# RWKV state chain as batched affine maps, chunk matrices of two heads in one loop, full-height lora products

## The chip, the cores and the metric

The kernel runs on one core of a Trainium2 chip. The metric is the device time of one execution in microseconds, the median of three runs. The profile is one more execution on the same core; its engines are named PE (matrix multiply), PEld (PE's weight loads), DVE, ACT and POOL (element-wise work) and SP (which issues the DMAs).

## The reference

Two layers over x of shape (1, 512, 1024). In each layer one projection of the normalised input is split among three token mixers: latent attention (8 heads), forgetting attention (8 heads) and RWKV-7 time mixing (8 heads of 64). Their gated outputs are projected, merged and added to x. The change lies in the RWKV mixer, whose core is a recurrence over the 512 positions with a 64 by 64 state for each head:

```python
def step(state, inp):
    r_t, w_t, k_t, v_t, kk_t, a_t = inp
    sa = jnp.einsum('bhvk,bhk->bhv', state, -kk_t)
    state = (state * w_t[:, :, None, :] + sa[..., None] * (kk_t * a_t)[:, :, None, :]
             + v_t[..., None] * k_t[:, :, None, :])
    return state, jnp.einsum('bhvk,bhk->bhv', state, r_t)
```

The decay w and the rate a come from two small products ("lora") with 64 inner values each; in the second layer v is mixed with the first layer's v through a third one with 32 inner values.

## The kernel before

Everything is written with features on the 128 partitions and the 512 positions along the free axis. The large products are made of 128 by 128 weights against 128x512 moving tiles in three passes (`mm3`: high by high, high by low, low by high, all float32r), and weights are split into high and low parts on ACT, DVE and POOL as they arrive. Each layer is written as five generators that are woven together: `rwkv_preps`, `rwkv_chains`, `attention`, `merge_gates`, `merge`. The instructions that come out of them are then put in an order by the function `plan`, which lists, for each engine, the instructions in the order in which the engine will issue them; it weighs the path that is left behind an instruction and prices of its own for each kind of instruction, waits and changes of PE's tile shape. Some copies may go to one of two or three engines, and `plan` picks. On the chip each engine keeps that order, so PE issues work of all five generators in turn, and a matmul that waits holds all that is listed behind it.

The RWKV mixer treats the heads in four pairs per layer (the index p; head 0 of a pair lies on partitions 0 to 63, head 1 on 64 to 127, `HS` names both halves) and the positions in 8 chunks of 64. `rwkv_front` makes decay and rate: `lora` multiplies the weights `ws` by `WA` with one product over 128 rows and one over 64 rows. `rwkv_inv` makes the chunk matrices `At` for each head and chunk (L979, 16 products of `KB0` and `KR` per pair, for one head after the other, in the PSUM bank `xk`) and inverts their triangular part into `W` (a loop on POOL, and 32-row products at L1020 and L1026). `rwkv_chain` then walks the chunks. In the stretches that the prediction reads, one chunk is

- R: `Rs` = At part of head h times values (L1056), plus `KR` times the state `Sh` (L1065, not in chunk 0),
- A: `W` times `Rs` (L1069), copied into `VSA` as two 64x64 pieces,
- S: `KBn` times `VSA` (L1075, not in chunk 7), from which the next state is made on DVE (L1077) with the scaled old state `sl`.

Each of R, A and S is one 64 by 64 product for each of the two heads, side by side in different halves of the array, and each needs the result of the one before it, through DVE or ACT. The outputs follow at the end: for each chunk L1087 (128 rows, 64 columns) and, from chunk 1 on, L1093 (64 by 64). All these operands are plain float32, and the profile counts two PE instructions ("passes") for each such product. The PSUM bank `ch` has one buffer, so its users follow one another.

Of the kernel before, what the change touches and what calls it, by code (L numbers as in the profile page):

```python
# [9 lines left out]
F32 = mybir.dt.float32  # L10
# [203 lines left out]
def plan(insts, tags, manual, flex, margin, replay=None):  # L214
# [79 lines left out]
    short = [op.kind == "InstMatmult" and op.cost < 107 for op in ops]  # L294
# [4 lines left out]
    def forward(follow=None):  # L299
# [11 lines left out]
        table, columns, last_pass, last_short = "exp", [(0, 128)], 0.0, False  # L311
        held = [(0.0, 0)] * 5
        mode, pe_end = (128, 128), 0.0
# [94 lines left out]
        for _ in ops:  # L408
# [14 lines left out]
            if op.kind == "InstMatmult":  # L423
                last_short = short[k]
                c0, c1 = op.outs[0][1:3]
                load = op.array[1] / 1.2
                ld = max(due(k, e), last_pass)
                if op.array != mode:
                    ld = max(ld, pe_end + DRAIN)
                    mode = op.array  # L430
                s = max(s, ld + load)
                if c1 - c0 <= 64 and all(c1 <= a or b <= c0 for a, b in columns):
                    cost = 20
                    columns.append((c0, c1))
                    last_pass = s
                else:
                    columns = [(c0, c1)]
                    last_pass = s + (0 if "float32r" in op.ins[0][7] or op.inst.is_transpose else cost / 2)
            start[k], free[e] = s, s + cost
            if e == PE:  # L440
                pe_end = max(pe_end, s + dict(op.costs)[e])
# [90 lines left out]
def build(tc, x_t, wpk, wsm, wv, vec, cst, out, order_of=None, pick={}, queues=None, margin=2.0):  # L532
# [184 lines left out]
    for l in range(L):  # L717
# [160 lines left out]
        def load_v(p):  # L878
            v = T(tag="vp", bufs=2)
            nc.sync.dma_start(v, vs[p])  # L880
            if l:
                vu, u = TX(), T(dt=F32R)[:, 0:256].rearrange("p (a c) -> p a c", a=2)
                nc.sync.dma_start(vu[64:128, 0:128], wv[l - 1, 64:128, 128 + 128 * p:256 + 128 * p])
                copy(u[64:128, 0, :], vu[64:128, 0:128])
                combine(u[64:96, 1, :], vu[64:96, 0:128], u[64:96, 0, :].bitcast(F32), ALU.subtract)
# [17 lines left out]
        def lora(ps, ws, i):  # L903

            pe.matmul(ps, ws[:, i, :], WA[:, i, :], start=True, stop=False)
            pe.matmul(ps, ws[HS[i], 2, :], WA[HS[i], i, :], start=False, stop=True)

        def rwkv_front(p):
# [4 lines left out]
            ws = T(dt=F32R)[:, 0:384].rearrange("p (i c) -> p i c", i=3)  # L913
            copy(ws[:, 0:2, :], raw[:, 0:256].rearrange("p (i c) -> p i c", i=2))
            for i, hs in enumerate(HS):
                combine(ws[hs, 2, :], raw[hs, 128 * i:128 * i + 128], ws[hs, i, :].bitcast(F32), ALU.subtract)
# [37 lines left out]
        def rwkv_inv(p, front, v):  # L954
# [19 lines left out]
            for h, hs in enumerate(HS):  # L974
                for g in range(2):
                    ps = PS("xk").rearrange("p (c t) -> p c t", t=128)
                    for c in range(4):
                        cc = 4 * g + c
                        pe.matmul(ps[:, c, :], KB0[hs, cc].rearrange("p a t -> p (a t)"),  # L979
                                  KR[hs, cc].rearrange("p a t -> p (a t)"), start=True, stop=True)  # L980
                    dve.tensor_tensor(At[:, h, 4 * g:4 * g + 4, :], ps,
                                      amask.unsqueeze(1).broadcast_to([128, 4, 128]), op=ALU.mult)
                    yield
# [47 lines left out]
        def rwkv_chain(p, ops):  # L1031
# [17 lines left out]
            built[0] += 1  # L1049
            Sh = rpool.tile([128, 8, 64], F32, name="Sh", tag="Sh", bufs=1)  # L1050
            for c in range(8):
                ps = PS("ch")
                pR, pA, pS = (ps[:, 64 * i:64 * i + 64] for i in range(3))
                Rs = T((128, 64), "Rs", 1)
                for h, hs in enumerate(HS):
                    pe.matmul(pR[hs], At[hs, h, c, 0:64], VSA[hs, c, hs], start=True, stop=c == 0)  # L1056
                if c:
                    if c < 7:
                        sl = T((128, 64), "sl", 1)
                        lc = lam[:, c:c + 1]  # L1060
                        any_of([(DVE, 162), (ACT, 240), (POOL, 472)], lambda q: act.activation(
                            sl, Sh[:, c, :], AF.Copy, scale=lc) if q == ACT else
                            (dve if q == DVE else gp).tensor_scalar(sl, Sh[:, c, :], lc, None, op0=ALU.mult))
                    for h, hs in enumerate(HS):
                        pe.matmul(pR[hs], KR[hs, c, 0, :], Sh[hs, c, :], start=False, stop=True)  # L1065
                copy(Rs, pR, DVE)
                yield
                for h, hs in enumerate(HS):
                    pe.matmul(pA[HS[1 - h]], W[hs, c, :], Rs[hs], start=True, stop=True)  # L1069
                for h, hs in enumerate(HS):  # L1070
                    copy(VSA[HS[1 - h], c, hs], pA[HS[1 - h]], DVE)
                yield
                if c < 7:
                    for h, hs in enumerate(HS):
                        pe.matmul(pS[hs], KBn[:, c, hs], VSA[:, c, hs], start=True, stop=True)  # L1075
                    if c:
                        dve.scalar_tensor_tensor(Sh[:, c + 1, :], pS, lam[:, c:c + 1], sl, op0=ALU.mult, op1=ALU.add)  # L1077
                    else:
                        dve.tensor_scalar(Sh[:, c + 1, :], pS, lam[:, c:c + 1], None, op0=ALU.mult)
                    yield  # L1080

            ps = PS("ch")
            last = [None, None]
            for c in range(8):
                cc = slice(64 * c, 64 * c + 64)
                for h, hs in enumerate(HS):
                    i1 = pe.matmul(ps[hs, cc], VSA[:, c, hs], At[:, h, c, 64:128], start=True, stop=c == 0)  # L1087
                    if c:
                        order(i1, last[h])
                    last[h] = i1  # L1090
                for h, hs in enumerate(HS):
                    if c:
                        last[h] = pe.matmul(ps[hs, cc], Sh[hs, c, :], KR[hs, c, 1, :], start=False, stop=True)  # L1093
# [640 lines left out]
```

## Time and profile before

| what | value |
|---|---|
| time, median of 3 runs | 1460.1 us (1458.55 to 1460.61) |
| time of the profiled execution | 1460.2 us |
| its span, first to last instruction | 1458.4 us |
| PE busy | 1409.8 us (97%), 7828 instructions |
| DVE busy | 1178.6 us (81%) |
| ACT busy | 787.9 us (54%) |
| POOL busy | 390.1 us (27%) |
| weight loads (PEld) busy | 1079.9 us (74%) |
| mean granted TensorE clock | 0.987 |
| DMA | 158.59 MB, mean 109 GB/s |

Busy time of PE counts a matmul from its start to its modelled end, and neighbours overlap: two 128x512 matmuls start 0.23 us apart and each lasts 0.39 us. What a piece of work costs PE is therefore read from starts: from the start of the matmul ahead of it to the start of the second matmul behind it, less what those two neighbours take when nothing lies between them.

### The profile page before, as it was taken

The numbers are of one execution on the slowest core, as the hardware profiler recorded it, in microseconds if no ns is written. First come the engines' busy times: TensorE is split into PE (matmuls) and PEld (weight loads), VectorE is DVE, ScalarE is ACT, GpSimd is POOL, SyncE is SP. The second block draws the span as 40 slices with busy tenths as digits, with TensorE's granted clock in tenths as the row PEclk, the third lists the DMA queues.
The fourth block names the chain that finished last, engine by engine and source line by source line (L and its number), as shares of the span: only waits on it lengthen the run. The fifth ranks groups of instructions, "written<-read, shape, count | busy, mean of one in ns | idle before, by whom it ended". The sixth has DMA issues, their size and how long they took to land. (4 is left out here: it accounts for less than half of the span.)

```text
span 1458.4 us, 23568 instructions
## 1 busy us (share of the span) xinstructions
PE 1409.8 (97%) x7828; PEld 1079.9 (74%) x7828; DVE 1178.6 (81%) x2787; ACT 787.9 (54%) x1653; POOL 390.1 (27%) x793
## 2 busy tenths in 40 slices
PE   7999999999999999999999999999989999999998
PEld 5677677676677777887877776777777676778887
DVE  8868878879887869878788778778688988688784
ACT  7546666546555546442254756457458567464330
POOL 1225260352440102112021251161252271012020
PEclk9999999999999999999999999999999999999999
DMA  5343123222333224555534332123232333254563
GB/s 172 109 120 105 44 59 88 80 62 84 94 80 116 88 79 139 166 184 166 184 116 130 93 97 65 55 64 103 84 95 58 122 85 95 66 174 152 164 211 102
DMA packets 114619, 158.59 MB, mean 109 GB/s; under 512 B 36544, under 2 KB 44608, under 8 KB 114496
## 3 DMA queue, kind: packets, MB, share of 16 engines
q1 hardware_dynamic: 114496, 157.08, 35.9%
q8 instruction: 62, 1.02, 0.3%
q14 instruction: 61, 0.50, 0.1%
HBM read 128.72 MB, written 28.31 MB: 108 GB/s over the span
## 5 line engine op out<-in xcount | busy, mean ns | idle before, releaser
L771 PE MATMUL acc<-hh,w 128*128 128x512 f32 x1008 | 377.9, 410 | 16.2 <-DVE w L651 5.4
L772 PE MATMUL acc<-hl,w 128*128 128x512 f32 x1008 | 375.6, 408 | 3.1 <-DVE hl L651 3.0
L773 PE MATMUL acc<-hh,w 128*128 128x512 f32 x1008 | 372.6, 406 | 0.0
L651 POOL TENSOR_TENSOR w<-raw,w 128x256 fp32r<-128x256 f32 (+1 forms) x152 | 130.7, 863 | 728.0 <-ACT w L639 337.9
L639 ACT ACTIVATE w<-raw 128x256 fp32r<-128x256 f32 (+1 forms) x341 | 138.0, 413 | 211.1 <-PE acc L773 137.3
L651 DVE TENSOR_TENSOR w<-raw,w 128x256 fp32r<-128x256 f32 (+1 forms) x548 | 233.4, 437 | 15.3 <-ACT w L639 9.9
L771 PEld LDWEIGHTS acc<-hh,w 128*128 128x128 f32 x1008 | 189.9, 191 | 60.8 <-ACT hh L639 10.8
L772 PEld LDWEIGHTS acc<-hl,w 128*128 128x128 f32 x1008 | 190.2, 190 | 46.4 <-DVE hl L651 5.7
L773 PEld LDWEIGHTS acc<-hh,w 128*128 128x128 f32 x1008 | 190.9, 190 | 42.7 <-issue 0.7
L639 DVE CAST w<-raw 128x256 fp32r<-128x256 f32 x359 | 104.2, 298 | 111.6 <-PE acc L773 84.6
L1000 POOL TENSOR_TENSOR W<-W,NL 128x60 f32<-128x60 f32 (+24 forms) x248 | 81.5, 329 | 76.2 <-DMA NL<-d 58.4
L1190 PE MATMUL wk<-qk 96*128 96x512 f32 (+10 forms) x320 | 98.2, 327 | 1.2 <-DVE qn L639 0.6
L1002 POOL TENSOR_TENSOR W<-W 128x60 f32<-128x60 f32 (+24 forms) x248 | 85.3, 344 | 18.2
L651 DVE TENSOR_TENSOR PP<-wk,PP 128x512 fp32r<-128x512 f32 (+3 forms) x128 | 61.7, 485 | 17.2 <-ACT PP L639 16.2
L1190 PEld LDWEIGHTS wk<-qk 128*128 128x128 f32 (+2 forms) x320 | 60.2, 191 | 13.7 <-DVE PP L651 2.2
L1165 DVE CUSTOM_DVE_ANT_0 wk<-wk,cmask 128x128 f32<-128x128 f32 (+3 forms) x128 | 61.3, 499 | 3.4 <-PE wk L1164 2.8
L1191 DVE TENSOR_TENSOR wk<-wk,dmask 128x128 f32<-128x128 f32 x128 | 38.3, 302 | 28.4 <-PE wk L1190 27.5
L639 ACT ACTIVATE KV<-ch 64x64 f32<-64x64 f32 (+2 forms) x135 | 40.2, 298 | 38.0 <-PE ch L1069 21.1
L639 ACT ACTIVATE PP<-wk 128x384 fp32r<-128x384 f32 (+3 forms) x95 | 41.7, 440 | 26.0 <-PE av L1204 23.7
L1218 DVE RECIPROCAL do<-do 128x512 f32<-128x512 f32 x16 | 53.5, 3343 | 0.1
L1195 ACT ACTIVATE wk<-wk,ncum 128x512 f32<-128x512 f32 (+1 forms) x64 | 31.5, 493 | 36.6 <-DVE wk L1191 36.5
L1164 PE MATMUL wk<-qk 96*128 96x384 f32 (+7 forms) x128 | 42.3, 345 | 5.9 <-DVE ty L1165 4.4
(518 smaller groups left out, 2891.9 us busy)
## 6 DMA issues: line engine op xcount, KB each, us to landing
raw<-wpk SPq DMA_DIRECT2D x326, 256.0 KB, 2.7
tx<-thd SPq DMA_DIRECT2D x54, 256.0 KB, 3.3
thd<-zth SPq DMA_DIRECT2D x48, 256.0 KB, 2.1
tx<-odr SPq DMA_DIRECT2D x22, 256.0 KB, 3.6
raw<-wpk SPq DMA_DIRECT2D x32, 128.0 KB, 2.3
NL<-d SPq DMA_DIRECT2D x32, 128.0 KB, 2.7
odr<-sg SPq DMA_DIRECT2D x14, 256.0 KB, 2.4
x<-x_t SPq DMA_DIRECT2D x8, 256.0 KB, 4.0
```

Of the source, the lines that this page charges most:

```text
L639: lambda q: act.activation(dst, src, AF.Copy) if q == ACT else dve.tensor_copy(dst, src))
L651: any_of(costs, lambda q: (dve if q == DVE else gp).tensor_tensor(dst, a, b, op=op))
L771: pe.matmul(ps, wh, xh, start=first, stop=False)
L772: pe.matmul(ps, wh, xl, start=False, stop=False)
L773: pe.matmul(ps, wl, xh, start=False, stop=last)
L1000: gp.tensor_tensor(tv, WL[:, 0:m, s:s + 1].broadcast_to([128, m, n]), NL[:, s:s + 1, s + 1:32].broadcast_to([128, m, n]), op=ALU.mult)
L1002: gp.tensor_tensor(WL[:, 0:m, s + 1:32], WL[:, 0:m, s + 1:32], tv, op=ALU.add)
L1164: pe.matmul(ps[:, 0:n], t[sr, A["sq"], 128 * i:n], t[sr, 2, 0:n], start=True, stop=True)
L1165: dve.tensor_tensor_reduce(out=ps[:, 0:n], in0=ps[:, 0:n], in1=cmask[:, 512 - n:512], scale=1.0, scalar=NEG, op0=ALU.add, op1=ALU.max, acc ...
L1190: pe.matmul(pv, t[rows, k, js], t[rows, q, q0:512], start=i == 0, stop=i == len(passes) - 1)
L1191: dve.tensor_tensor(ps[:, js], ps[:, js], dmask, op=ALU.add)
L1218: dve.reciprocal(dn, dn)
```

## The change

In the chain, the walk over chunks is replaced by seven batches of 16 products (8 chunks times 2 heads, helper `each`, L1056), all without the state: a transposed `KR` (`KT`); R without the state; M = W times KT; W times R into `VSA`; Q (the output map, added to `KR`'s second half); `KBn` times `VSA`, scaled, into `G`; and M times `KBn`, which with the identity added overwrites `KBn` as a map of both heads with zeros outside the two diagonal blocks. After each batch a 512-wide copy or DVE operation empties the bank `ch`. Then the state goes through six products of 128 by 128 by 64 (L1095), each followed by one DVE operation, and the outputs are 16 products (L1102) followed by 14 (L1106) with no order forced between chunks. Per pair that is 112 + 6 + 30 = 148 products for 30 + 16 + 14 + 30 = 90.

In `rwkv_inv` the loop for the chunk matrices takes both heads of a chunk one after the other, head 0 into the bank `xk` and head 1 into `ch`. In `lora` and `load_v` the low parts of the weights are kept at full height, so that both products have the same number of rows. In `plan` the price of a product beside others of a smaller tile shape goes from 20 to 6 and counts rows too, and the start of a weight load changes.

```diff
@@ plan, forward @@
-                ld = max(due(k, e), last_pass)
+                ld = last_pass if due(k, e) <= last_start else max(due(k, e), last_pass)
...
-                if c1 - c0 <= 64 and all(c1 <= a or b <= c0 for a, b in columns):
-                    cost = 20
-                    columns.append((c0, c1))
-                    last_pass = s
+                r0, r1 = op.ins[0][1:3]
+                if op.array != (128, 128) and all(c1 <= a or b <= c0 or r1 <= p or q <= r0 for a, b, p, q in beside):
+                    cost = 6
+                    beside.append((c0, c1, r0, r1))
@@ load_v @@
-                pe.matmul(ps, u[64:96, 1, :], vd[64:96], start=False, stop=True)
+                pe.matmul(ps, u[64:128, 1, :], vd[64:128], start=False, stop=True)
@@ lora @@
-            pe.matmul(ps, ws[:, i, :], WA[:, i, :], start=True, stop=False)
-            pe.matmul(ps, ws[HS[i], 2, :], WA[HS[i], i, :], start=False, stop=True)
+            for a in range(2):
+                pe.matmul(ps, ws[:, a, i, :], WA[:, i, :], start=a == 0, stop=a == 1)
@@ rwkv_inv @@
-            for h, hs in enumerate(HS):
-                for g in range(2):
-                    ps = PS("xk").rearrange("p (c t) -> p c t", t=128)
-                    for c in range(4):
-                        cc = 4 * g + c
-                        pe.matmul(ps[:, c, :], KB0[hs, cc].rearrange("p a t -> p (a t)"),
-                                  KR[hs, cc].rearrange("p a t -> p (a t)"), start=True, stop=True)
+            for g in range(2):
+                two = [PS(tag).rearrange("p (c t) -> p c t", t=128) for tag in ("xk", "ch")]
+                for c in range(4 * g, 4 * g + 4):
+                    for h, hs in enumerate(HS):
+                        pe.matmul(two[h][:, c % 4, :], KB0[hs, c].rearrange("p a t -> p (a t)"),
+                                  KR[hs, c].rearrange("p a t -> p (a t)"), start=True, stop=True)
@@ rwkv_chain @@
+            def each(ps, out, lhs, rhs):
+                for c in range(8):
+                    for h, hs in enumerate(HS):
+                        pe.matmul(ps[out(h), c, :], lhs(h, c), rhs(h, c), start=True, stop=True)
...
+            ps = chunks()
+            each(ps, same, lambda h, c: At[HS[h], h, c, 0:64], lambda h, c: VSA[HS[h], c, HS[h]])
+            copy(R, ps)
+            yield
...
+            ps = chunks()
+            each(ps, same, lambda h, c: KBn[:, c, HS[h]], lambda h, c: VSA[:, c, HS[h]])
+            dve.tensor_tensor(G, ps, lam.unsqueeze(2).broadcast_to([128, 8, 64]), op=ALU.mult)
+            yield
...
+            for c in range(1, 7):
+                ps = PS("ch")[:, 0:64]
+                pe.matmul(ps, KBn[:, c, :], state[c], start=True, stop=True)
+                dve.scalar_tensor_tensor(state[c + 1], ps, lam[:, c:c + 1], G[:, c, :], op0=ALU.mult, op1=ALU.add)
+                yield
```

What this moves on PE shows at two places. The first is the first head pair's chunk matrices. PE's order before has the products (L979, four at a time, from `KR` and `KB0` into `xk`) between large projections:

```order
L771 MATMUL acc<-hh,w 128x512 x2
L979 MATMUL xk<-KR,KB_760 128x128 x4
L771 MATMUL acc<-hh,w 128x512
L772 MATMUL acc<-hl,w 128x512 x2
L773 MATMUL acc<-hh,w 128x512 x2
L979 MATMUL xk<-KR,KB_760 128x128 x4
L771 MATMUL acc<-hh,w 128x512 x2
```

and now, where `xk` is head 0 and `ch` is head 1:

```order
L770 MATMUL acc<-hh,w 128x512
L974 MATMUL ch<-KR,KB_761 128x128 x2
L974 MATMUL xk<-KR,KB_761 128x128 x4
L974 MATMUL ch<-KR,KB_761 128x128 x2
L770 MATMUL acc<-hh,w 128x512
L771 MATMUL acc<-hl,w 128x512
L770 MATMUL acc<-hh,w 128x512
L771 MATMUL acc<-hl,w 128x512 x2
L974 MATMUL xk<-KR,KB_761 128x128 x3
L974 MATMUL ch<-KR,KB_761 128x128
L974 MATMUL xk<-KR,KB_761 128x128
L974 MATMUL ch<-KR,KB_761 128x128 x3
```

Eight products now stand together where four did, and the two heads stand in blocks, not in turn.

The second place is the walk over chunks. PE's order before has, for one chunk of the last chain, R (L1056 and L1065), A (L1069) and S (L1075), each of two products or two and two, between attention (L1190, L1202) and projections:

```order
L1056 MATMUL ch<-KV,At 64x64 x2
L1065 MATMUL ch<-Sh,KR 64x64 x2
L772 MATMUL acc<-hl,w 128x512
L773 MATMUL acc<-hh,w 128x512
L1190 MATMUL wk<-qk_11877 128x128
L773 MATMUL acc<-hh,w 128x512
L1069 MATMUL ch<-Rs,W 64x64 x2
L1190 MATMUL wk<-qk_11877 128x128
L1190 MATMUL wk<-qk_11955 128x512
L771 MATMUL acc<-hh,w 128x512 x2
L1190 MATMUL wk<-qk_11955 128x512
L1075 MATMUL ch<-KV 64x64 x2
```

and now, for all chunks of the second pair's chain in the first layer:

```order
L1056 MATMUL ch<-KR,W 64x64 x16
L1204 MATMUL wk<-qk_446 128x128
L1217 MATMUL av<-PP,Vl 64x384
L1204 MATMUL wk<-qk_446 128x128
L1218 MATMUL av<-PP,Vh 128x384
L771 MATMUL acc<-hl,w 128x512
L1216 MATMUL av<-PP,Vh 128x256
L1056 MATMUL ch<-At,W 64x64 x16
L1217 MATMUL av<-PP,Vl 64x256
L772 MATMUL acc<-hh,w 128x512
L1218 MATMUL av<-PP,Vh 128x256
L770 MATMUL acc<-hh,w 128x512
```

Sixteen products stand together, with some six wide matmuls between one batch and the next. Over the whole program PE leaves its full tile shape for a smaller one 288 times before and 147 times now (a count over the two orders).

## Rows read from the trace of the kernel before

**Rows 1.** The page's first part: busy time of each engine.

```profile
PE 1409.8 (97%) x7828; PEld 1079.9 (74%) x7828; DVE 1178.6 (81%) x2787; ACT 787.9 (54%) x1653; POOL 390.1 (27%) x793
```

**Rows 2.** Span and mean granted clock of the core.

```profile
core 0: 1458.4 us, clock 0.987
```

**Rows 3.** Timeline of PE, 1237 to 1239.5: start us, us, instruction, count.

```profile
1237.17 0.39 PE L1190 MATMUL wk<-qk 128*128 128x512 f32 x1
1237.49 0.34 PE L1075 MATMUL ch<-KV 128*64 128x64 f32 x4
1237.76 0.50 PE L772 MATMUL acc<-hl,w 128*128 128x512 f32 x1
1238.10 0.34 PE L1202 MATMUL av<-PP,Vh 128*128 128x384 f32 x1
1238.27 0.40 PE L772 MATMUL acc<-hl,w 128*128 128x512 f32 x1
1238.60 0.33 PE L1056 MATMUL ch<-KV,At 64*64 64x64 f32 x4
1238.76 0.28 PE L1065 MATMUL ch<-Sh,KR 64*64 64x64 f32 x4
1238.97 0.51 PE L773 MATMUL acc<-hh,w 128*128 128x512 f32 x1
1239.32 0.34 PE L1203 MATMUL av<-PP,Vl 128*64 128x384 f32 x1
```

**Rows 4.** Timeline of PE, 48.9 to 50.6: projections and a lora product.

```profile
48.96 0.39 PE L772 MATMUL acc<-hl,w 128*128 128x512 f32 x1
49.19 0.39 PE L905 MATMUL xk<-WA,tx 128*128 128x512 f32 x1
49.41 0.40 PE L771 MATMUL acc<-hh,w 128*128 128x512 f32 x1
49.74 0.49 PE L906 MATMUL xk<-WA,tx 64*128 64x512 f32 x1
50.16 0.50 PE L772 MATMUL acc<-hl,w 128*128 128x512 f32 x1
50.50 0.86 PE L773 MATMUL acc<-hh,w 128*128 128x512 f32 x3
```

**Rows 5.** Timeline of PE, 1167.6 to 1172.4: a chain's outputs.

```profile
1167.68 0.39 PE L1190 MATMUL wk<-qk 128*128 128x512 f32 x1
1167.99 0.45 PE L1087 MATMUL ch<-At,KV 128*64 128x64 f32 x8
...
1171.80 0.74 PE L772 MATMUL acc<-hl,w 128*128 128x512 f32 x2
1172.38 0.40 PE L773 MATMUL acc<-hh,w 128*128 128x512 f32 x1
```

**Rows 6.** Timeline of PE, 141.8 to 142.5: a batch of 32-row products.

```profile
141.82 0.69 PE L1020 MATMUL xk<-NL,At 32*32 32x32 f32 x32
142.47 0.33 PE L1164 MATMUL wk<-qk 96*128 96x128 f32 x1
```

**Rows 7.** Timeline of PE, 177.3 to 178.9: four chunk matrices of one head.

```profile
177.37 0.28 PE L1190 MATMUL wk<-qk 97*128 97x256 f32 x1
177.58 1.16 PE L979 MATMUL xk<-KR,KB 64*128 64x128 f32 x8
178.67 0.33 PE L1190 MATMUL wk<-qk 96*128 96x128 f32 x1
178.83 0.39 PE L1202 MATMUL av<-PP,Vh 128*128 128x384 f32 x1
```

**Rows 8.** PE groups by form: count, busy us, mean ns, idle before.

```profile
L1075 PE MATMUL ch<-KV 128*64 128x64 f32 x224 | 21.6, 248 | 3.2 <-DVE KV L639 2.2 <-ACT KV L639 1.0
```

**Rows 9.** ACT groups by form, copies out of the bank `ch`.

```profile
L639 ACT ACTIVATE KV<-ch 64x64 f32<-64x64 f32 x92 | 20.0, 218 | 22.4 <-PE ch L1069 21.1 <-DVE tx L949 0.3
L639 ACT ACTIVATE KV<-ch 128x512 f32<-128x512 f32 x18 | 10.7, 596 | 13.1 <-PE ch L1093 12.2 <-PE ch L1039 0.7
```

More of the change, by code (lines that the diff above doesn't have):

```diff
@@ L292, in plan @@
         op.urgency = max(way, default=0) + (600 if op.dma else op.cost)
-    short = [op.kind == "InstMatmult" and op.cost < 107 for op in ops]
     opens = defaultdict(list)
@@ L440, in forward @@
             if e == PE:
+                last_start = s
                 pe_end = max(pe_end, s + dict(op.costs)[e])
@@ L912, in rwkv_front @@
             nc.sync.dma_start(raw[:, 0:256], wsm[l, :, 256 * p:256 * p + 256])
[L913 to L916, printed above, removed]
+            ws = T(dt=F32R).rearrange("p (a i c) -> p a i c", a=2, i=2)
+            split(raw[:, 0:256].rearrange("p (i c) -> p i c", i=2), ws[:, 0], ws[:, 1])
             if p:
@@ new lines, in rwkv_chain @@
+            same, swap = (lambda h: HS[h]), (lambda h: HS[1 - h])
+            ps = chunks()
+            each(ps, same, lambda h, c: KR[HS[h], c, 0, :], lambda h, c: C["ident"][HS[h], HS[h]])
+            copy(KT, ps)
+            yield
[3 more added lines that the diff above has]
+            yield
+            ps = chunks()
+            each(ps, swap, lambda h, c: W[HS[h], c, :], lambda h, c: KT[HS[h], c, :])
@@ new lines, in rwkv_chain @@
+            copy(M, ps)
+            yield
+            ps = chunks()
+            each(ps, swap, lambda h, c: W[HS[h], c, :], lambda h, c: R[HS[h], c, :])
+            for h, hs in enumerate(HS):
+                copy(VSA[HS[1 - h], :, hs], ps[HS[1 - h]])
+            yield
+            ps = chunks()
+            each(ps, same, lambda h, c: M[HS[1 - h], c, :], lambda h, c: At[HS[1 - h], h, c, 64:128])
+            dve.tensor_tensor(Q, ps, Q, op=ALU.add)
+            yield
+            ps = chunks()
@@ new lines, in rwkv_chain @@
+            each(ps, same, lambda h, c: KBn[:, c, HS[h]], lambda h, c: VSA[:, c, HS[h]])
+            dve.tensor_tensor(G, ps, lam.unsqueeze(2).broadcast_to([128, 8, 64]), op=ALU.mult)
+            yield
+            ps = chunks()
+            each(ps, same, lambda h, c: M[HS[1 - h], c, :], lambda h, c: KBn[HS[1 - h], c, HS[h]])
+            for h, hs in enumerate(HS):
+                fill(KBn[hs, :, HS[1 - h]], 0.0)
+                dve.tensor_tensor(KBn[hs, :, hs], ps[hs], C["ident"][hs, hs].unsqueeze(1).broadcast_to([64, 8, 64]),
+                                  op=ALU.add)
@@ L1053, in rwkv_chain @@
-                pR, pA, pS = (ps[:, 64 * i:64 * i + 64] for i in range(3))
-                Rs = T((128, 64), "Rs", 1)
                 for h, hs in enumerate(HS):
[L1056 to L1065, printed above, removed]
@@ L1066, in rwkv_chain @@
-                copy(Rs, pR, DVE)
-                yield
-                for h, hs in enumerate(HS):
[L1069 to L1093, printed above, removed]
+                    pe.matmul(ps[hs, 64 * c:64 * c + 64], VSA[:, c, hs], At[:, h, c, 64:128], start=c == 0, stop=c == 0,
+                              skip_group_check=True)
@@ L1095, in rwkv_chain @@
+            for c in range(1, 8):
+                for h, hs in enumerate(HS):
+                    pe.matmul(ps[hs, 64 * c:64 * c + 64], state[c][hs], Q[hs, c, :], start=False, stop=True,
+                              skip_group_check=True)
             yo = VSA.rearrange("p c t -> p (c t)")
```

21 lines of the change are left out of this document (13 added, 8 removed).

## The prediction

> **What bounds the kernel.** I read the page's busy times first: PE is busy for 1409.8 of 1458.4 us, DVE for 81%, everything else far less [rows 1, 2]. PE is idle for only 48.6 us, so PE's own list of work sets the time, and what this change is worth is what it takes off that list. Busy time does not say what a small product costs, since it overlaps with its neighbours; the timeline of PE does. Where only wide matmuls follow each other, a 128x512 one starts 0.23 us after the last one (48.96 to 49.19 to 49.41), and narrower ones take in proportion: 0.17 for 384 columns (1238.10 to 1238.27) [rows 3, 4]. Against that I read what PE loses when it leaves the full tile shape and comes back, which I call a stop. At 1237.17 to 1238.10 stand one wide matmul, the two products of S (four passes) and one more wide matmul: 0.93 us, less twice 0.23, is 0.47 us for a stop with four passes. R, with eight passes, takes 1239.32 - 1238.27 - 0.46 = 0.59 us [rows 3]. So two further products of 64 by 64, side by side, cost 0.12 us, and the stop itself costs 0.35 us before it has done anything: a late start, a drain, and the next wide matmul's weights, loaded late (it starts the following one 0.34 us later, not 0.23). The 90 products of a pair are spread over many such stops, and there are 8 pairs.
>
> **Chain, before.** Over 8 pairs: R is 8 stops of four passes and 56 of eight, 8 x 0.47 + 56 x 0.59 = 36.8 us; A is 64 x 0.47 = 30.1; S is 56 x 0.47 = 26.3. A chain's outputs, uninterrupted, take 1172.38 - 1167.68 - 3 x 0.23 = 4.01 us [rows 5], times 8 is 32.1. Together 125 us. The order shows that some groups are cut in two (20 more stops, 0.35 us each, 7 us) and that outputs stand in 23 stops, not 8 (15 x 0.2, 3 us, since they change shape there anyway). Before: 135 us.
>
> **Chain, after.** Sixteen products in one stop are 32 passes: 0.47 + 7 x 0.12 = 1.31 us. That a long run keeps this pace is seen in the 32-row products, whose 32 passes take 0.65 us, drain included [rows 6]. 56 batches cost 73.4 us. The six state products use the full shape, so they make no stop. A plain float32 product of that shape is not in the trace; the nearest row is L979, also 128 columns of weights, 1.09 us for 8 passes with the drain [rows 7], some 0.11 us a pass, hence 0.22 us for two passes. The bounds are 0.12 (as two wide matmuls of 64 columns would be, at the pace of rows 4) and 0.47 (a stop). I take 0.22, because the weights are as wide as L979's: 48 x 0.22 = 10.6 us, between 6 and 23. Outputs: 1.31 for the first 16, then a change of shape and 14 more. In rows 5 the groups after the first of eight cost (4.01 - 0.59) / 13 = 0.26 each, so 0.26 + 6 x 0.12 = 0.98; together 2.29, times 8 is 18.3. The order keeps 52 of the 56 batches whole and cuts four into 27 pieces: 23 x 0.35 = 8 us. After: 110 us. **Gain 25 us.** The 464 added products thus cost less than the stops that go.
>
> **Chunk matrices.** A stop with eight passes of L979 takes 178.83 - 177.37 - 0.12 - 0.06 = 1.28 us [rows 7], of which 0.35 is the stop: 0.116 us a pass. Before, 128 products stand in 43 stops: 256 x 0.116 + 43 x 0.35 = 44.7 us. If the heads really ran side by side, each pair of passes would cost one, and 16 stops with 128 steps would be 20.4 us, 24 less. But the order does not alternate them: it puts up to four products of one head, then up to four of the other, in 25 runs, and only 26 neighbours belong to different heads. In this trace passes of one tile follow each other at that 0.11, and PE starts matmuls in the order of its list. So 25 x 0.35 + 256 x 0.116 - 26 x 0.116 = 35.4 us, a **gain of 9**, of which 6 comes from fewer stops.
>
> On this place the Trainium skill speaks twice. "TensorEngine Tiling (Array Packing)", Key Properties, has different tiles load and multiply in parallel; by that alone the gain would be the 24 us above. "TensorE: Matmul & The Clock Gate", Part 3, has matmuls start and end strictly in program order, by which blocks of one head overlap with the other only at their edges; the rows agree with it, and the sum goes by the order.
>
> **Lora.** L906 (64 rows) between full ones makes a stop: 50.50 - 49.41 - 0.46 = 0.63 us [rows 4]. At full height it takes 0.23: 16 x 0.40 = **6.4 us gained**. In load_v the second product (32 rows) gets the first one's shape, but they stand together only twice out of four times: **1 us gained**. The 32-row products of the inverse are cut into 27 runs instead of 20: 7 x 0.35 = **2.4 us lost**.
>
> **Waits.** The chain's copies hold PE up now: 3.2 us before S alone [rows 8]. A batch's reader is longer, 0.60 us for 128x512 against 0.22 for a 64x64 copy [rows 9], and holds the single bank `ch`, but each reader stands for eight chunks, and between batches the order places mostly four to seven wide matmuls, about 1 us, which covers a copy of 0.60 and two semaphore crossings. If that cover failed by half, 56 batches would wait 0.3 us each, 17 us; the lower bound is that all of today's waits before R, A and S go, 7 us by S's row with R and A alike or less. I take 3 us gained. DVE and ACT have fewer instructions (134 and 114 less by the orders), so DVE, at 81%, gets no nearer to being the bound than the shorter span itself brings it.
>
> **Sum.** 25 + 9 + 6.4 + 1 - 2.4 + 3 = 42 us off the profiled execution's own 1460.2 us (its span is 1458.4, 1.8 lie around it; the median of the runs is 1460.1, so it is a fair one): **1418 us**. Its own range, with the state products at 0.12 or 0.47, waits between 7 gained and 10 lost, and the cuts half or double: 1402 to 1435.
>
> **Rivals.** First, the batches wait: thirteen steps of a chain depend on each other through one bank. The chain's slots must then be filled by others, and where the list puts little between two batches, PE stands still. For it: readers three times as long. Against it: the cover counted above. At 0.5 us for each of 56 batches 28 us go: about 1444. The Trainium skill, "TensorEngine Tiling (Array Packing)", PSUM Bottleneck, warns of this: faster small products leave the copying out of PSUM as the limit. Here copying gets less in number, and that rule alone would move the time by no more than this rival.
>
> Second, the gain is larger: the core's clock is granted at 0.987 on average [rows 2]; 1.3% of 1458 is 19 us lost at 1.2 instead of 2.4 GHz. If fewer stops and waits halve that, and edges of heads overlap better than counted, 10 + 8 us come on top: 1400.
>
> Third, nothing is gained: the time PE is freed from comes back as waits for DVE, whose list (1178.6 us) is the next longest. It would have to be the bound in the stretches with RWKV work; PE would then be idle for about 42 us more. About 1460.
>
> Fourth, it gets slower, by the clock: batches of narrow products and six thin state products per chain could let the clock fall more often. Each us at 1.2 GHz loses half a us. Before, 38 us of the span stood at the low level (1.3% doubled); to eat 42 us the low stretches would have to grow by 84 us, to three times as much, about 10 us more for each chain. From there on it is slower: with 100 us more, 1468. Against it: wide matmuls stand between the batches, and the outputs, a dense run of narrow products, get shorter.
>
> **How the numbers follow.** The forecast gets 0.58, the larger gain 0.16, waiting batches 0.14, nothing gained 0.05, slower 0.07. The predicted time is the forecast's, 1418. A range of 1395 to 1446 takes in the larger gain and the waiting batches and leaves out some 0.15. A change under 0.2% (3 us) can't be told from none. Faster: 0.58 + 0.16 + 0.14 = 0.88; same 0.05; slower 0.07.
>
> **What would show it.** In the profile after, a batch of 32 passes at L1056 should take about 1.3 us between its wide neighbours; if it takes 2 or more, the pace of long runs was misread. The state products at L1095 should cost near 0.22 us each with no stop. L974 should show blocks at 0.11 us a pass with little overlap; alternating starts a few ns apart would make the gain there larger. L904 should start 0.23 us after its neighbour. PE's idle total should stay near 45 us; idle time before L1056 growing past 15 us would be the waiting batches, and a mean clock below 0.96 the slower case. The prediction is wrong at its root if PE stops being the engine that is always busy.

## The result, and the profile after

| | median us | lowest to highest | ratio to the kernel before, 95% interval |
|---|---|---|---|
| before | 1460.36 | 1458.55 to 1463.63 | |
| changed | 1415.28 | 1414.39 to 1419.28 | 0.9694 [0.9669, 0.9719] |

The changed kernel takes 45 us less, 3.1%. The forecast was 1418. It lies that near in part by luck: the sum priced the list some us too high and had no term for the clock, and the two errors nearly cancel.

The page's first part and the span with the granted clock, of the changed kernel (as rows 1 and 2 have them of before):

```profile
PE 1367.5 (97%) x8756; PEld 1085.1 (77%) x8756; DVE 1171.3 (83%) x2653; ACT 777.3 (55%) x1539; POOL 452.8 (32%) x875
```

```profile
core 0: 1413.5 us, clock 0.995
```

PE is still the engine that is always busy: 1413.5 - 1367.5 leaves 46.0 us idle, where it was 48.6 [rows 1]. So the time came off PE's own list, and not out of waits, although the list has 928 instructions more. The second number to see is the clock. (1 - clock) x span is what the low level costs, an estimate from the rounded mean: 19.0 us before [rows 2], 7.1 now. By that some 12 of the 45 us are clock, and only 33 are the list. The estimate takes rather too much off: over the 33 executions of the kernel before that were timed beside the experiments, all with one and the same list, a us more of it came with only 0.66 us more of span. By that slope 8 us are clock and 37 the list.

PE's groups by form (count, busy us, mean ns, idle before) show that the batches do not wait:

```profile
L1056 PE MATMUL ch<-KV,At 64*64 64x64 f32 x512 | 18.4, 221 | 0.4 <-DVE At L977 0.3
L1056 PE MATMUL ch<-cs,KR 64*64 64x64 f32 x256 | 15.5, 226 | 0.4 <-DVE KV L638 0.4
L1095 PE MATMUL ch<-Sh,KV 128*128 128x64 f32 x80 | 14.0, 256 | 1.8 <-DVE Sh L1096 1.7
```

The other groups of L1056 have no idle time. All batches together wait 0.8 us, and the state products 1.8, where the products of S alone waited 3.2 [rows 8].

Timeline of PE, changed kernel: a batch of 16 products, a state product, and a chain's outputs (start us, us, instruction, count):

```profile
179.32 0.39 PE L770 MATMUL acc<-hh,w 128*128 128x512 f32 x1
179.64 1.15 PE L1056 MATMUL ch<-KV,At 64*64 64x64 f32 x32
180.72 0.50 PE L771 MATMUL acc<-hl,w 128*128 128x512 f32 x1
181.06 0.28 PE L1204 MATMUL wk<-qk 96*128 96x256 f32 x1
...
183.69 0.39 PE L772 MATMUL acc<-hh,w 128*128 128x512 f32 x1
183.92 0.33 PE L1095 MATMUL ch<-At,KV 128*128 128x64 f32 x2
184.06 0.48 PE L772 MATMUL acc<-hh,w 128*128 128x512 f32 x1
184.37 0.22 PE L1204 MATMUL wk<-qk 96*128 96x128 f32 x1
...
499.67 0.39 PE L770 MATMUL acc<-hh,w 128*128 128x512 f32 x1
499.99 1.15 PE L1102 MATMUL ch<-At,KV 128*64 128x64 f32 x32
501.07 0.33 PE L1106 MATMUL ch<-KR,At 64*64 64x64 f32 x4
501.24 0.87 PE L1106 MATMUL ch<-KR,Sh 64*64 64x64 f32 x24
502.03 0.50 PE L772 MATMUL acc<-hh,w 128*128 128x512 f32 x1
502.37 0.40 PE L771 MATMUL acc<-hl,w 128*128 128x512 f32 x1
```

Read as the prediction read rows 3: from the start of the wide product ahead to the start of the second behind, less 0.46. The batch costs 181.06 - 179.32 - 0.46 = 1.28 us (forecast 1.31), the state product 184.37 - 183.69 - 0.46 = 0.22 (0.22; the median of all 48 is 0.23) with its wide neighbours on their 0.23 pace, the outputs 502.37 - 499.67 - 0.46 = 2.24 (2.29). The full-height lora product, as rows 4 showed its half-height forerunner:

```profile
48.47 0.39 PE L771 MATMUL acc<-hl,w 128*128 128x512 f32 x1
48.70 0.39 PE L904 MATMUL xk<-WA,tx 128*128 128x512 f32 x1
48.92 0.40 PE L772 MATMUL acc<-hh,w 128*128 128x512 f32 x1
```

It starts 0.23 us after its neighbour and holds nobody up: 0.23 for 0.63, as forecast.

One reading differs. The first pair's chunk matrices are those whose order, listed above with the change, has `xk` x3, `ch`, `xk`, `ch` x3 (products of two passes each):

```profile
73.20 0.62 PE L771 MATMUL acc<-hl,w 128*128 128x512 f32 x2
73.76 0.60 PE L974 MATMUL xk<-KR,KB 64*128 64x128 f32 x3
74.09 0.37 PE L974 MATMUL ch<-KR,KB 64*128 64x128 f32 x1
74.20 0.27 PE L974 MATMUL xk<-KR,KB 64*128 64x128 f32 x1
74.30 0.27 PE L974 MATMUL ch<-KR,KB 64*128 64x128 f32 x1
74.31 0.27 PE L974 MATMUL xk<-KR,KB 64*128 64x128 f32 x1
...
75.18 0.97 PE L772 MATMUL acc<-hh,w 128*128 128x512 f32 x3
75.98 0.62 PE L770 MATMUL acc<-hh,w 128*128 128x512 f32 x2
```

By the list the first `ch` pass stands behind six `xk` passes; it starts (74.09) ahead of the fourth (74.20), and from there the heads run side by side. The run costs 75.98 - 73.20 - 5 x 0.23 = 1.63 us; the prediction's count (0.35, and 0.116 for each of 16 passes less the three places where the heads change) makes 1.86. Of the ten runs of 16 passes the cheapest cost 1.62, the median 1.86 and the dearest 2.14, in which six passes of one head start alone, then two pairs, then six of the other. So PE kept the list's order within a head, and not strictly between the two halves of its rows; that each engine keeps its list, as said of the kernel before, holds for PE with this exception. "TensorE: Matmul & The Clock Gate", Part 3, of the Trainium skill has starts strictly in program order; these starts do not agree with it, and the prediction was wrong to follow it to the letter.

### The profile page after: what moved, and what is told of

The parts are those of the page before. It is cut to its first block, busy times and chain, and to the rows that moved or that the text cites. A ratio compares the mean times of both kernels' runs of the same rounds, so it can differ in the third digit from the quotient of the medians.

```text
span 1413.5 us, 25288 instructions
## 1 busy us (share of the span) xinstructions
PE 1367.5 (97%) x8756; PEld 1085.1 (77%) x8756; DVE 1171.3 (83%) x2653; ACT 777.3 (55%) x1539; POOL 452.8 (32%) x875
## 5 line engine op out<-in xcount | busy, mean ns | idle before, releaser
L770 PE MATMUL acc<-hh,w 128*128 128x512 f32 x1008 | 371.0, 405 | 15.6 <-DVE hh L638 5.1
L650 POOL TENSOR_TENSOR w<-raw,w 128x256 fp32r<-128x256 f32 (+1 forms) x215 | 180.4, 845 | 626.9 <-DVE w L638 292.1
L772 PE MATMUL acc<-hh,w 128*128 128x512 f32 x1008 | 369.8, 404 | 5.3 <-DVE w L650 5.1
L771 PE MATMUL acc<-hl,w 128*128 128x512 f32 x1008 | 366.8, 402 | 1.1 <-DVE hl L650 0.9
L638 ACT ACTIVATE w<-raw 128x256 fp32r<-128x256 f32 (+1 forms) x367 | 147.4, 413 | 247.6 <-PE acc L772 137.9
L772 PEld LDWEIGHTS acc<-hh,w 128*128 128x128 f32 x1008 | 189.6, 190 | 45.1 <-DVE w L650 5.6
L650 DVE TENSOR_TENSOR w<-raw,w 128x256 fp32r<-128x256 f32 x485 | 207.7, 441 | 8.0 <-ACT w L638 3.3
L638 DVE CAST w<-raw 128x256 fp32r<-128x256 f32 (+1 forms) x333 | 98.6, 304 | 98.8 <-PE acc L772 78.6
L996 POOL TENSOR_TENSOR W<-W,NL 128x60 f32<-128x60 f32 (+24 forms) x248 | 88.1, 355 | 72.6 <-DMA NL<-d 55.4
L1204 PE MATMUL wk<-qk 96*128 96x512 f32 (+7 forms) x320 | 99.1, 324 | 1.0 <-ACT vt L638 0.6
L638 ACT ACTIVATE PP<-wk 128x512 fp32r<-128x512 f32 (+3 forms) x93 | 39.8, 435 | 28.5 <-PE av L1218 24.8
L1216 PE MATMUL av<-PP,Vh 128*128 128x512 f32 (+3 forms) x128 | 42.3, 330 | 0.5 <-ACT do L638 0.2
```

The source lines that it names most:

```text
L638: lambda q: act.activation(dst, src, AF.Copy) if q == ACT else dve.tensor_copy(dst, src))
L650: any_of(costs, lambda q: (dve if q == DVE else gp).tensor_tensor(dst, a, b, op=op))
L770: pe.matmul(ps, wh, xh, start=first, stop=False)
L771: pe.matmul(ps, wh, xl, start=False, stop=False)
L772: pe.matmul(ps, wl, xh, start=False, stop=last)
L996: gp.tensor_tensor(tv, WL[:, 0:m, s:s + 1].broadcast_to([128, m, n]), NL[:, s:s + 1, s + 1:32].broadcast_to([128, m, n]), op=ALU.mult)
```

## The experiments

Each kernel ran four times (e2 and e3 ten times) beside the kernel before, whose median was then 1460.1 to 1461.7. "At full clock" is span x mean clock of the profiled run, an estimate of what the list would take with no low clock; between executions of one kernel it differs by 1 to 10 us, so a few us in it say little. The profiled run of e13 is its fastest; the other three had clocks of 0.967 to 0.977. Stops are counted in PE's order. PE's idle time, where it is named below, is the profiled span less PE's busy time.

| kernel | median us (lowest to highest) | ratio, 95% interval | clock | at full clock | stops |
|---|---|---|---|---|---|
| before | 1460.4 | | 0.987 | 1439 | 288 |
| changed | 1415.3 | 0.9694 [0.9669, 0.9719] | 0.995 | 1406 | 147 |
| e1_old_chain | 1449.6 (1449.2 to 1451.0) | 0.9929 [0.9905, 0.9953] | 0.991 | 1434 | 268 |
| e2_chain_only | 1458.6 (1452.8 to 1463.2) | 0.9983 [0.9962, 1.0004] | 0.982 | 1434 | 210 |
| e3_more_stops | 1460.6 (1458.6 to 1467.0) | 1.0004 [0.9981, 1.0027] | 0.980 | 1429 | 197 |
| e4_heads_in_turn | 1412.6 (1412.2 to 1414.0) | 0.9675 [0.9652, 0.9699] | 0.996 | 1405 | 157 |
| e5_old_prices | 1439.6 (1437.1 to 1442.5) | 0.9850 [0.9802, 0.9898] | 0.988 | 1420 | 164 |
| e8_replanned | 1433.9 (1428.1 to 1441.5) | 0.9813 [0.9761, 0.9864] | 0.980 | 1405 | 152 |
| e9_ahead_of_batch | 1437.3 (1430.5 to 1439.7) | 0.9825 [0.9779, 0.9872] | 0.985 | 1412 | 145 |
| e10_hold_shape | 1416.6 (1415.6 to 1418.2) | 0.9692 [0.9654, 0.9730] | 0.990 | 1402 | 122 |
| e11_stops_same_plan | 1436.8 (1435.9 to 1437.6) | 0.9838 [0.9820, 0.9856] | 0.992 | 1423 | 201 |
| e12_ahead_same_plan | 1422.6 (1421.2 to 1422.9) | 0.9739 [0.9721, 0.9757] | 0.992 | 1410 | 149 |
| e13_before_replanned | 1474.3 (1463.2 to 1484.8) | 1.0119 [1.0075, 1.0163] | 0.986 | 1441 | 307 |
| e14_replanned_too | 1438.9 (1436.6 to 1441.5) | 0.9853 [0.9832, 0.9875] | 0.985 | 1413 | 145 |

**One part undone.** e1 puts the old walk over chunks back into the changed kernel; e2 puts back the old loop for the chunk matrices, `lora` and `load_v` instead, so that only the chain is new.

```diff
@@ e1, rwkv_chain @@
-            each(ps, same, lambda h, c: At[HS[h], h, c, 0:64], lambda h, c: VSA[HS[h], c, HS[h]])
...
+            for c in range(8):
...
+                    pe.matmul(pR[hs], At[hs, h, c, 0:64], VSA[hs, c, hs], start=True, stop=c == 0)
@@ e2, rwkv_inv and lora @@
-                two = [PS(tag).rearrange("p (c t) -> p c t", t=128) for tag in ("xk", "ch")]
+            for h, hs in enumerate(HS):
...
-                pe.matmul(ps, ws[:, a, i, :], WA[:, i, :], start=a == 0, stop=a == 1)
+            pe.matmul(ps, ws[HS[i], 2, :], WA[HS[i], i, :], start=False, stop=True)
```

> The walk over chunks of the kernel before stands again in the changed kernel; chunk matrices, lora products and the planner's prices stay as changed. Theory of stops: the list has 268 stops where the changed kernel has 147, and the chain was priced at 25 us; so some 25 us come back: 1440 us. Rival, the clock does much of it: the profile after shows 16 us at the low clock where before had 39, some 11 us of the gain; if that goes with the chain, 11 us more come back, 1451 us, and the mean granted clock falls to 0.987. Rival, the chain is worth little and the other parts carry the gain: under 1425 us.

> Only the chain is changed (with the planner's new prices); chunk matrices and lora products are those of the kernel before. Theory of stops, with the parts priced one by one: 9 + 6.4 + 1 us come back, 1432 us. But the list has 210 stops, not 147: 16 of them lora products, about 18 more the chunk matrices, and some 30 because batches are now cut into pieces. If every stop counts 0.35 us and more, 63 of them are at least 22 us: 1437 to 1450 us. If the parts simply add, 1432; if stops decide, the later figure.

Neither part is worth by itself what was expected: the chain alone gains 2 to 3 us (by the interval, between none and 6) and the rest alone 12, where both together gain 45. Of the 34 us that e1 lies above the changed kernel, 28 remain at full clock, near the 25 of the sum; but PE also idles longer in e1's plan (54.8 us, for 46.0), so that 19 are left for its list. The timeline of PE of e2 (its batch is L1059, its lora L904 and L905) shows one reason:

```profile
985.61 0.33 PE L1059 MATMUL ch<-KR,W 64*64 64x64 f32 x2
985.93 0.50 PE L904 MATMUL xk<-WA,tx 128*128 128x512 f32 x1
986.35 0.33 PE L1059 MATMUL ch<-KR,W 64*64 64x64 f32 x2
986.61 0.49 PE L905 MATMUL xk<-WA,tx 64*128 64x512 f32 x1
987.03 1.03 PE L1059 MATMUL ch<-KR,W 64*64 64x64 f32 x28
```

The planner cuts batches in two and three: in e2 only 34 of 56 are whole (119 pieces), in the changed kernel 52 (79 pieces). Each cut is a stop more. So undoing a part also makes a new plan, and its cuts and its clock (0.982) hide what the part does. Why e2's plan cuts more is not shown.

**Two stops for each batch, and the same product without a stop.** e3 puts one constant product of full tile shape, which the batch overwrites, into the middle of each of the 56 batches, and so splits them; e9 puts the same product ahead of each batch.

```diff
@@ each, e3 @@
                 for c in range(8):
+                    if c == 4:
+                        pe.matmul(ps[:, 4:6, :], CR["bd"], CR["ones"], start=True, stop=True)
                     for h, hs in enumerate(HS):
@@ each, e9 @@
+                pe.matmul(ps[:, 4:6, :], CR["bd"], CR["ones"], start=True, stop=True)
                 for c in range(8):
```

> The changed kernel with one full-shape product of two constants (128 columns) put in the middle of each of the 56 batches; its result is overwritten by the batch. Theory of stops: each such product divides a batch into two stops, and the list has 197 stops where the changed kernel has 147; 50 stops at 0.35 us and 56 products at 0.06 us are 21 us: 1436 us. Rival, what counts is PE's passes and not the change of tile shape: 56 times 0.06 is 3 us, 1418 us.

> The same 56 full-shape products of constants as in the run with more stops, but ahead of each batch and not in its middle: as much added work, and 145 stops, as in the changed kernel with 147. Theory of stops: 56 products at 0.06 to 0.11 us, 3 to 6 us: 1418 to 1422 us. Rival, added work in the chain and its waits cost as much wherever it stands: 1440 to 1460 us, as with more stops.

e3 loses all of the gain, much more than its 50 stops were to cost. But e9, with two stops less than the changed kernel, also loses 22 us, and its clock is 0.985. The difference of the two, 23 us, is near the price of the stops; either one alone also contains another plan. That made the next two necessary.

**The same two, with the plan held.** The product is left out while the plan is made and put into PE's list afterwards, directly ahead of the next product of its batch. Every engine's list is otherwise word for word the changed kernel's.

```diff
@@ each: e11; e12 has c == 0 @@
+                    if c == 4 and queues is not None:
+                        extra.append(pe.matmul(ps[:, 4:6, :], CR["bd"], CR["ones"], start=True, stop=True).ins.name)
@@ after plan @@
+    for k in added:
+        queues[PE].insert(queues[PE].index(k + 1), k)
```

> As the run with more stops, but every engine keeps the changed kernel's own list, word for word, and the 56 full-shape products of constants are put into PE's list in the middle of the batches. 201 stops instead of 149 with the products ahead. Theory of stops: 54 x 0.35 + 56 x 0.06 = 22 us more than the changed kernel, 1437 us, at the same clock (0.995); if the clock falls as it did in the run with more stops (0.980), up to 20 us on top. Rival, the earlier 45 us came from the new plan and not from stops: under 1425 us.

> The changed kernel's own lists again, with the 56 products of constants ahead of the batches: 149 stops. Theory of stops: 56 products at 0.06 to 0.11 us, 3 to 6 us, 1418 to 1421 us; the 22 us that the run with the products ahead lost against the changed kernel were then the plan's and the clock's. Rival, added products in the chain cost 0.4 us each wherever they stand: 1437 us.

Timelines of PE, e11 and then e12 (the batch is L1058), at the same batch:

```profile
168.38 0.25 PE L772 MATMUL wk<-w,cqh 128*128 128x192 f32 x1
168.56 0.68 PE L1058 MATMUL ch<-KV,At 64*64 64x64 f32 x16
169.18 0.33 PE L1056 MATMUL ch<-ones,bd 128*128 128x128 f32 x1
169.43 0.68 PE L1058 MATMUL ch<-KV,At 64*64 64x64 f32 x16
170.04 0.36 PE L770 MATMUL wk<-w,cqh 128*128 128x192 f32 x1
170.24 0.30 PE L772 MATMUL wk<-w,ckh 128*128 128x256 f32 x1
```

```profile
168.78 0.26 PE L772 MATMUL wk<-w,cqh 128*128 128x192 f32 x1
168.87 0.24 PE L1056 MATMUL ch<-ones,bd 128*128 128x128 f32 x1
169.04 1.15 PE L1058 MATMUL ch<-KV,At 64*64 64x64 f32 x32
170.12 0.36 PE L770 MATMUL wk<-w,cqh 128*128 128x192 f32 x1
170.31 0.30 PE L772 MATMUL wk<-w,ckh 128*128 128x256 f32 x1
```

From L772 to the same L772 behind it, e11 takes 170.24 - 168.38 = 1.86 us and e12 170.31 - 168.78 = 1.53: the stop costs 0.33 here, by the same work on both sides. Of the 56 batches, 52 stand between the same neighbours in both traces. Read there in the same way, the stop costs 0.28 to 0.35 us in 45 of them and 0.12 to 0.17 in seven, where in e12 the constant product itself started 0.10 to 0.54 us late; the median is 0.34, the mean 0.31, the sum 16.0 us. Over the program, 52 stops more cost 1436.8 - 1422.6 = 14.2 us, 0.27 each (13.0 to 16.3 us between the single runs), at the same mean clock (0.992). The page's first part, e11 and then e12, shows where the rest went:

```profile
PE 1391.5 (97%) x8812; PEld 1103.6 (77%) x8812; DVE 1173.2 (82%) x2653; ACT 778.5 (54%) x1539; POOL 451.0 (31%) x875
PE 1374.9 (97%) x8812; PEld 1096.6 (77%) x8812; DVE 1173.1 (83%) x2653; ACT 777.7 (55%) x1539; POOL 451.2 (32%) x875
```

With spans of 1434.4 and 1421.1 us PE idles 42.9 us in e11 and 46.2 in e12, 3.3 less with the stops: a little of what the stops cost takes the place of waits. This is the cleanest result of the study: an added stop costs 0.34 us at the typical place, where the prediction had 0.35, and 0.27 net over the program. The 56 full-shape products ahead of the batches cost 1422.6 - 1415.3 = 7.3 us, 0.13 each, with two stops more and a lower clock; at full clock (1410 against 1406) it is about half of that. The drain at a change of tile shape that the Trainium skill names ("TensorEngine Tiling (Array Packing)", Key Properties, without a price) is what these rows agree with.

**The same work in another plan.** `MARGINS`, two numbers of the planner, (1.7, 1.5) so far, are changed a little: in the changed kernel twice, in the kernel before once.

```diff
@@ e8 and e13; e14 has (1.75, 1.55) @@
-MARGINS = (1.7, 1.5)
+MARGINS = (1.65, 1.45)
```

> The changed kernel, only planned anew: the two stretch factors for waits are 1.65 and 1.45 instead of 1.7 and 1.5, and the list comes out with 152 stops instead of 147. It measures what a new plan alone does to the time. Stops: 2 us, 1417 us. If waits and the clock come out differently by chance of the plan, as the profiles of the earlier runs suggest, up to 15 us either way: 1400 to 1430 us.

> The kernel before, planned anew with stretch factors 1.65 and 1.45. Its list has 307 stops instead of 288: by the theory of stops 7 us more, 1467 us. What a plan does by chance to waits and clock was 16 us in the changed kernel planned anew, so 1450 to 1480 us. If it came below 1440, most of the change's gain would be a matter of the plan.

> The changed kernel, planned anew with stretch factors 1.75 and 1.55; 145 stops instead of 147, so the list itself is worth 1416 us. A second sample of what the plan and the clock add by chance: 1408 to 1436 us, and the mean granted clock should say where in that: near 0.995 at the lower end, near 0.980 at the upper.

The work is the same, and the time moves by up to 24 us. At full clock e8 equals the changed kernel (1405 and 1406); by that estimate its whole loss of 19 us is clock, 28.7 us of it against 7.1, and by the slope of 0.66 some 14 of the 19 are. Where one part of that comes from, the timeline of PE of e8 shows (idle time and who ended it in brackets), and beneath it the stretch behind it, from the busy times by window of e8 and of the changed kernel (columns: us, busy us and count of PE, PEld, DVE, ACT, POOL, then granted clock, DMA share, GB/s):

```profile
882.45 0.50 PE L1216 MATMUL av<-PP,Vh 128*128 128x512 f32 x1 [2.75 <-ACT PP L638]
...
883.25 0.39 PE L770 MATMUL acc<-hh,w 128*128 128x512 f32 x1
884.53 0.79 PE L887 MATMUL xk<-tx 64*128 64x512 f32 x1 [0.89 <-DVE tx L650]
```

```profile
883.40:903.90 20.50, 19.61 (x68) 14.35 (x67) 12.32 (x24) 3.69 (x9) 0.32 (x2) 0.51 0.21 59
```

```profile
883.40:903.90 20.50, 20.36 (x276) 17.05 (x275) 14.13 (x31) 10.35 (x24) 9.70 (x29) 1.00 0.21 53
```

PE stands still for 2.75 us because ACT is late with `PP`; four wide products later comes another wait, and then a 64-row product of 512 columns lasts 0.79 us, where its like lasted 0.49 [rows 4]: PE is at the low level (1.2 GHz, half of 2.4) for 20 us, in which by the estimate 10 us are lost. In the same stretch of the changed kernel the clock is 1.00. The sequence is shown, a wait and then the fall; that the wait is its cause is a likely reading, which no run here tested. It is not the only way in: in the kernel before the clock also fell in the middle of a chain's outputs, without any wait of PE in the 6 us ahead (busy times by window, columns as above):

```profile
193.00:199.60 6.60, 6.60 (x67) 4.62 (x65) 4.58 (x15) 2.19 (x7) 5.19 (x19) 1.00 0.10 25
199.60:206.40 6.80, 6.80 (x36) 5.53 (x36) 4.22 (x15) 3.34 (x8) 5.11 (x15) 0.50 0.00 1
```

e14 loses at both ends (7 us at full clock, where PE idles 54.2 us for 46.0, and 14 to the clock), and e13 is 14 us slower than the kernel before in the median, with runs up to 1485. So the change is worth 26 to 36 us at full clock in the five plans of the two kernels (1439 and 1441 against 1405, 1406 and 1413), and in the medians each plan of the changed kernel (1415, 1434, 1439) is faster than each plan of the one before (1460, 1474). What the clock added to the 45 us belongs at least in large part to this plan, the best of the three, and not to the change; whether shorter outputs gave some of it is not shown.

**The planner's prices.** e5 leaves the new work and puts the old prices of small products back.

```diff
@@ e5, plan @@
-                if op.array != (128, 128) and all(c1 <= a or b <= c0 or r1 <= p or q <= r0 for a, b, p, q in beside):
-                    cost = 6
+                if c1 - c0 <= 64 and all(c1 <= a or b <= c0 for a, b in columns):
+                    cost = 20
```

> The changed kernel planned with the prices of the kernel before (20 for a product beside another one, rows not counted, the older start of a weight load). The list has 164 stops instead of 147, with 40 lone products of the chain cut out of their batches. Theory of stops: 17 stops more, about 8 us: 1423 us. Rival, the prices carry the gain: 1440 us or more. Rival, they do nothing: 1412 to 1418 us.

24 us are lost, 14 of them at full clock, with 17 more stops and only 47 of the 56 batches whole. PE idles 54.5 us, 8.5 more than in the changed kernel, and 17 stops at 0.31 would be 5: together the 14. In the median that is no more than e14's plan loses by its margins, though at full clock it is twice as much, so the prices as a cause are not separated from the plan.

**The heads strictly in turn, and fewer stops.** e4 forces the products of the chunk matrices to alternate between the heads; e10 adds to e4 a higher limit up to which the planner keeps PE at its present tile shape (`PE_WAIT` 8000 for 2000).

```diff
@@ e4, rwkv_inv @@
+                        turn_ = pe.matmul(two[h][:, c % 4, :], KB0[hs, c].rearrange("p a t -> p (a t)"),
...
+                        if h or c % 4:
+                            order(turn_, was)
+                        was = turn_
@@ e10, besides @@
-PE_WAIT = 2000
+PE_WAIT = 8000
```

> The changed kernel with the chunk matrices' products held in the order head 0, head 1, head 0, head 1; the order puts 127 neighbours of different heads side by side where the changed kernel has 26 inside its runs. Theory that PE follows its list: a run of 16 passes falls from 1.8 us (seen after) to 0.35 + 8 x 0.12 = 1.3 us, some 8 us in all: 1407 us. Rival, the two row halves already run past each other whatever the order inside a run, so that only the cuts matter: 1413 to 1418 us.

> Heads in turn as before, and the planner holds PE's tile shape longer (it takes a product of the present shape over one of another shape if that is less urgent by up to 8000 and not 2000 of its units). The list has 122 stops instead of 157. Theory of stops: 35 stops at 0.4 us, 14 us less than with heads in turn: 1398 us. Rival, work that is urgent waits too long behind the held shape, PE idles more and the clock falls: 1412 to 1430 us.

Timeline of PE, e4, the first pair's chunk matrices:

```profile
72.23 0.39 PE L770 MATMUL acc<-hh,w 128*128 128x512 f32 x1
72.56 0.37 PE L974 MATMUL xk<-KR,KB 64*128 64x128 f32 x1
72.57 0.37 PE L974 MATMUL ch<-KR,KB 64*128 64x128 f32 x1
...
73.66 0.50 PE L771 MATMUL acc<-hl,w 128*128 128x512 f32 x1
73.99 0.39 PE L770 MATMUL acc<-hh,w 128*128 128x512 f32 x1
```

Sixteen passes cost 73.99 - 72.23 - 0.46 = 1.30 us: in turn, the heads run fully in parallel, two passes for the price of one. e4 is the fastest kernel of the study, 2.7 us under the changed one; the two intervals overlap, so it is no proven improvement. It gained less than the 8 us expected, since the list in blocks already overlapped and e4's plan has ten stops more. e10 saves 35 stops against e4, which by the price above should be 11 us, but only 3 us at full clock: PE idles 54.5 us, where it idled 47.7 in e4. The clock (0.990 for 0.996) takes more than that back, and e10 ends 4 us slower than e4. So the rival of the expectation held, PE idling more and the clock lower.

## Why the prediction was right, and where its sum was not

**Right.** PE's list is the bound, before and after: its idle time hardly moved. Stops are what the change saves on it: their price is shown by e11 against e12 with the plan held, and that the 141 stops which went had the same price is inferred. Where the time went can be read from the two traces: summed over every stretch in which one of the changed products stands, from the product ahead to the second behind, less the pace of the full-shape products in it, they took 232 us before and take 192 now, waits and low clock included. So 40 of the 45 us lie there. The batch, the state product, the outputs and the lora product cost at their places what the sum said (1.28, 0.22, 2.24 and 0.23 us), so the terms "chain after" and "lora" stand in the main; all 48 state products together took 15.8 us for 10.6, waits included. The two small terms, load_v and the 32-row products, were not measured apart. A batch cut at two passes costs even more than the 0.35: the median of the 21 pieces of two passes is 0.56. The wait for the batches did not come, nor DVE as the bound: L1056 waited 0.8 us for 56 batches, and PE's idle time stayed at 46.0, near the 45 given.

**Right in size, wrong in its ground: chunk matrices.** "PE starts matmuls in the order of its list" failed; the rows that were to agree with it showed one head's products alone [rows 7] and could not have shown otherwise. The step gave 9 us. Summed from each pass's start to the start behind it, the products took 37.3 us before (L979) and take 30.2 now (L974), 7 less; each of the 18 stops that went had besides a late start and a late second product behind it, 0.10 and 0.11 us by the rows of e4: 4 us, so 11 in all. What the list's blocks left on the table is seen in e4, where the same sum is 24.1 us: in a run that is not cut, strict alternation brings two passes for the price of one (1.30 us for sixteen).

**Missing from the sum: the clock.** It had no term for it; halving its 19 us stood only in the rival of the larger gain. Here 8 to 12 us came from it. e8 and e14 show that much of this is the plan's doing: with the same work the clock costs 29 and 22 us there.

**Mis-sized: the stop over a whole plan.** At full clock the list gained 33 us, by the slope of 0.66 it gained 37, and in any case not 42. The stretches summed above give 36 of it (227 and 190 us, when each us at the low clock is counted as half). No single place reads wrong, but with the plan held a stop is worth 0.31 us on average over its places and 0.27 net over the program, not 0.35; for 141 stops that is 6 or 11 us less, 36 or 31 instead of 42, close to what was measured. That this is the cause is worked out, not shown: the price was measured on stops put into the batches of the changed kernel, not on the stops of the kernel before.

**Slips in the working, without weight in the result.** At the pace of rows 4 two matmuls of 64 columns take 0.06 us, not the 0.12 that is the lower bound of the state product. The bounds that are named do not add up to 1402 and 1435: the state products (4 to 5 us less, 12 more), the waits (4 less, 13 more) and the cuts (4 less, 8 more) give 1405 to 1451. And 28 us more than the forecast is 1446, not 1444.

**Rivals.** "The batches wait" and "nothing gained" are refuted by the idle times above. "Slower by the clock" did not happen, but the clock can cost that much: e2, e3 and e8 lose 26 to 29 us to it, against 19 before. That batches and thin products bring the fall, as that rival had it, is not shown. "The larger gain" was half right, clock and overlap both, and the list's smaller gain took that back.

**Open.** Why one plan leaves a wait of some us at a place and another does not; and what the chunk loop and the lora part are worth separately, which was not tried. Undoing a part under a planner doesn't settle it, as e1 and e2 show.

## What to carry to other kernels

On an engine that is always busy, count how often it leaves its full tile shape and price that from starts of neighbouring instructions: here 148 small products in place of 90 for each head pair were worth it, because PE makes half as many stops. Where a planner decides the order, a variant that is planned anew measures the plan as well as the edit: hold the order and insert, or plan the same work several times, before a difference of some 20 us in 1400 is believed. And read the granted clock beside every span.

## What the runs showed of the hardware

PE starts passes on its two row halves out of the list's order (74.09 before 74.20, above), here by three passes; side by side, two passes of 128 weight columns take the 0.11 us of one (sixteen in 1.30 us, e4). Leaving the full tile shape and coming back costs 0.34 us at the typical place (e11 against e12). A wait of 2.75 us, and one of 0.89 soon after, were followed by 20 us at the low clock level (0.51); in the kernel before, the same level came at 199.6 us with no wait of PE in the 6 us ahead. And plans of the same work differ by 24 us (1415, 1434, 1439), more than most single edits here.
